# Small copies on VectorE in a two-layer hybrid attention block: products from PSUM, gathers on ScalarE

## The chip, the cores and the metric

One core of one Trainium2 chip runs the whole program. The metric is the time of one execution on the device in microseconds (us); the profile beside it comes from one further execution of the same program. Five engines work side by side, each through its own instructions in order: TensorE (PE, with PEld for its weight loads), VectorE (DVE), ScalarE (ACT), GpSimd (POOL) and SyncE (SP), which issues weight transfers.

## The reference

A block of two layers works on 272 tokens of width 1024, of which the first 16 ("meta" tokens) are prepended. Each layer has a mixer with three kinds of heads, and a feed-forward part:

```python
h = concatenate([meta, x])                      # 16 + 256 tokens, width 1024
for l in range(2):
    u = rmsnorm(h, norm_mix[l])
    qa, ka, va, qi, ki, wi, qb, kb, vb, qc, kc, vc, gc = split(u @ w_in[l])
    # a: 8 heads; an indexer (qi, ki, wi) picks the top 64 keys of each query; softmax; p @ va
    # b: 4 heads; two softmaxes of 32-wide halves, w = p0 - lam * p1; w @ vb; rmsnorm
    # c: 4 heads; rotary, then retention in chunks with decay; rmsnorm; times silu(gc)
    h = h + concatenate([a_out, b_out, c_out]) @ w_out[l]
    u = rmsnorm(h, norm_ff[l])
    h = h + square(relu(u @ w_ff1[l])) @ w_ff2[l]
return rmsnorm(h, final_norm)[:, 16:]
```

## The kernel before

The work is cut into units of one 1024x128 block of weights: per layer 31 units for w_in, 8 for w_out, 32 and 32 for the feed-forward part. One unit is one `slot`: 24 matmuls of 256 or 272 columns into one of four PSUM banks (`mm`). Each weight block comes by a transfer on SyncE's queue into `raw` (three buffers, five units ahead), is rounded by ScalarE into `hi` (L167, three units ahead), and the rest `raw - hi` goes into `lo` (L179, two units ahead), on VectorE or, for the units of `POOL_LO`, on GpSimd. The activations are split in the same way (`uh`, `ul`), so that each product is three matmuls (L186 to L188).

Everything else is set by hand into the gaps between the unit's matmuls. A slot has six places (evac, none, quarter, half, most, all); `PLACES` and `AFTER` give for each small function the slot and the place at which its instructions are put, as slot times six plus place. On each engine the instructions run in the order in which they are put.

Tokens lie along the columns; a tile of 128 partitions by 272 columns holds two heads of 64 (or four halves of 32). The first 16 columns belong to the meta tokens, and all heads' work on them is put together in block-diagonal form:

- `e_mul` (L464, L466) and `b_split` (L471) turn PSUM into `ka`, `qa`, `kb`, `qb` by the row factor `bcast[key]` (tile bc). In the first layer, `meta_softmax` has three steps: `one` copies the first 16 columns of each head into its block of `kmA` or `kmB` (L577, tiles cleared once on GpSimd at L352); `two` multiplies with the queries, adds the bias, and takes minimum, difference (L592) and exponential; `three` divides by the sum (L601).
- `e_v` makes `vt` from PSUM (L475) and copies the first 16 columns into the blocks of `vbdT` (L477, L478). `e_v2` transposes vt on TensorE (L487) and ScalarE empties the bank (L488).
- `e_rot` makes the rotated `kr` and `qr` (L500, L503 on VectorE, the sum at L504 on GpSimd), and `e_kbd` copies kr's first columns into the blocks of `kbdT` (L507, L508), which `c_meta` multiplies with qr (L760).
- `b_pair`, `b_norm`, `b_keys` and `b_keys2` run the b heads: softmax parts (VectorE L554, L555, ScalarE L557, L558), sums and their inverse (L706, L707), a scaling on GpSimd (tile bp, L709), the difference on VectorE (L714), then a copy of the map's columns for meta keys into `wm` (L720), and the transposes (L563) with ScalarE's copy of the bank (L564).
- `i_head`, `i_round` and `i_mask` (L538, L544, L546, L550) find the top 64 on VectorE. `a_bias` adds mask and bias on GpSimd (L617, L618), `a_pair` multiplies (L627), `a_norm` scales on ScalarE (L640), `a_keys` copies the meta columns into `pm` (L649) and transposes.
- `e_ki` makes `kf` (L429), a rounded copy `kh` of it by a cast (L430), and the rest (L433).

Of the kernel before, what the change touches and what calls it, by code (L numbers as in the profile page):

```python
# [8 lines left out]
F = mybir.dt.float32  # L9
R = mybir.dt.float32r  # L10
AF = mybir.ActivationFunctionType
OP = mybir.AluOpType
# [5 lines left out]
T = SEQ + NM  # L18
# [8 lines left out]
N_UNITS = N_IN + N_OUT + N_F1 + N_F2  # L27

C_ID, C_ONES, C_COS, C_SIN, C_NEG, C_DEC, C_DECM, C_EXP = 0, 128, 256, 528, 800, 1072, 2608, 2880
C_ALL = 2896  # L30
P_MIX, P_FF, P_DN, P_RN = 0, 16, 32, 34
P_ALL = 38

# [4 lines left out]
PLACES = {  # L38
    "i_head": (28, 28, 34, 39, 45, 44, 52, 45),
    "i_round": (55, 57, 62, 64, 74, 77, 86, 91),  # L40
    "i_mask": (101,),
    "b_pair": (70, 87),
    "b_norm": (78, 79, 92, 98),
    "b_keys": (80, 83, 93, 101),
    "b_keys2": (88, 90, 100, 109),
    "a_bias": (104, 104, 107, 113, 131, 132, 140, 145),
# [6 lines left out]
    "r_scale": (123, 179),  # L53
    "r_out": (130, 181),
    "rot_tables": (99,),
    "e_kbd": (146, 157),
    "c_pair": (158, 163),
    "c_meta": (162,),
    "a_meta": (169,),
    "e_wi2": (16,),  # L60
    "b_first": (91,),
    "b_soft": (76, 84, 86),
    "a_soft": (124, 130, 136),
    "a_pv": (175, 181, 187, 195),
    "factor": (11, 12, 17),
}

AFTER = {
# [29 lines left out]
def block_kernel(ctx: ExitStack, tc: tile.TileContext, W, hin, cst, onehot, rbe, par, fin, dlam, out):  # L98
    nc = tc.nc
    ctx.enter_context(tc.manual_schedule())  # L100
    V, S, G, PE = nc.vector, nc.scalar, nc.gpsimd, nc.tensor
# [5 lines left out]
    small = ctx.enter_context(tc.tile_pool(name="small", bufs=3))  # L107
# [113 lines left out]
    cs = const.tile([128, C_ALL], F, name="cs")  # L221
# [3 lines left out]
    z = const.tile([128, 128], F, name="z")  # L225
# [21 lines left out]
    dec = cs[:, C_DEC:C_DEC + 1536].rearrange("p (h c) -> p h c", h=4)  # L247
    decm = cs[:, C_DECM:C_DECM + T]
    nhalf = cs[:, C_EXP:C_EXP + 16]

    nb = const.tile([128, 12, T], F, name="nb")
    vbdT = const.tile([128, 8, 128], F, name="vbdT")
    kbdT = const.tile([128, 2, 32], F, name="kbdT")
    kmA = const.tile([128, 4, 32], F, name="kmA")
    kmB = const.tile([128, 2, 64], F, name="kmB")
    smT = const.tile([128, 2, T], F, name="smT")
# [37 lines left out]
    bcast = {}  # L294
# [53 lines left out]
    at(13, "all", late_constants)  # L348

    def clear():  # L350
        for z in (vbdT, kbdT, kmA, kmB, smT[64:128]):
            G.memset(z, 0.0)  # L352
        G.memset(ss, 1.0)

# [54 lines left out]
    def meta_cols(x):  # L409
        return x[:, 0:288].rearrange("p (t c) -> p t c", t=2)[:, :, 0:16]  # L410

    def mixer(l):
# [3 lines left out]
        first = l == 0  # L416
        st = {}
        key = ("bc", l)
        factor_to_rows(b, key, 0, False)

        def e_ki(ps):
            bc = bcast[key]
            f = ta("kf")
            k2 = ck([128, 2, T], R, "ki")
            kh, kl = k2[:, 0], k2[:, 1]
            V.tensor_tensor(f[64:128], ps[64:128, :T], bc[64:128], OP.mult)  # L429
            V.tensor_copy(kh[64:128], f[64:128])  # L430
            S.activation(kh[0:64], f[64:128], AF.Copy)
            for r in (slice(64, 128), slice(0, 64)):
                V.tensor_tensor(kl[r], f[64:128], kh[64:128].bitcast(F), OP.subtract)  # L433
            st["ki"] = kh, kl
# [23 lines left out]
        def e_mul(ps, name, m, n, n0, scale=None):  # L458
            bc = bcast[key]
            if name not in st:  # L460
                st[name] = ck([128, n, T], F, name)
            o = st[name][:, m, n0:]
            if scale is None:
                V.tensor_tensor(o, ps[:, n0:T], bc[:, n0:], OP.mult)  # L464
            else:
                V.scalar_tensor_tensor(o, ps[:, n0:T], scale, bc[:, n0:], OP.mult, OP.mult)  # L466

        def b_split(ps, name, m, n0, scale):
            if name not in st:
                st[name] = ck([128, 2, T], F, name)  # L470
            V.scalar_tensor_tensor(st[name][:, m, n0:], ps[:, n0:T], scale, bcast[key][:, n0:], OP.mult, OP.mult)  # L471

        def e_v(ps, name, c0, vs):
            vt = ta("vt")
            V.tensor_tensor(vt, ps[:, :T], bcast[key], OP.mult)  # L475
            c = 32 * (vs if vs < 4 else vs % 2)
            V.tensor_copy(vbdT[0:64, vs, c:c + 16], vt[0:64, 0:16])  # L477
            V.tensor_copy(vbdT[64:128, vs, c + 16:c + 32], vt[64:128, 0:16])  # L478
            st["vt", vs] = vt

        def e_v2(name, c0, vs):
# [14 lines left out]
        def e_rot(ps, name, m, n0):  # L496
# [5 lines left out]
                i, o = 32 * q, 32 * (q ^ 1)  # L502
                V.tensor_tensor(y[o:o + 32, n0:], ps[i:i + 32, n0:T], st["sinr"][i:i + 32, n0:], OP.mult)  # L503
            G.tensor_tensor(st[name][:, m, n0:], x[:, n0:], y[:, n0:], OP.add)  # L504

        def e_kbd(m):
            V.tensor_copy(kbdT[0:64, m, 0:16], st["kr"][0:64, m, 0:16])  # L507
            V.tensor_copy(kbdT[64:128, m, 16:32], st["kr"][64:128, m, 0:16])  # L508

        def e_gate(ps, m):  # L510
            if m == 0:
# [51 lines left out]
                PE.transpose(pt[:, a * 128:a * 128 + 128], p[:, c:c + 128], ident)  # L563
            S.activation(dst, pt[:, :384], AF.Copy)  # L564

        def meta_softmax(name, plan, q, k, km, bias):

            tiles = km.shape[1]
            per = 8 // tiles
            rows = 128 // per  # L570
            x = {}

            def one():
                for i in range(tiles):
                    for a in range(per):
                        r = slice(rows * a, rows * a + rows)
                        V.tensor_copy(km[r, i, 16 * a:16 * a + 16], st[k][r, i, 0:16])  # L577

            def two():
                ps = att()  # L580
                for i in range(tiles):
                    PE.matmul(ps[:16, i * per * 16:(i + 1) * per * 16], st[q][:, i, 0:16], km[:, i, :],
                              start=True, stop=True)
                t = ta("mt", (16, 8, 16))
                if bias.ndim == 4:
                    V.tensor_tensor(t.rearrange("p (h a) c -> p h a c", a=2),
                                    ps[:16, :128].rearrange("p (h a c) -> p h a c", a=2, c=16), bias, OP.add)
                else:
                    V.tensor_tensor(t, ps[:16, :128].rearrange("p (h c) -> p h c", c=16), bias, OP.add)
                mn = small.tile([16, 8], F, name="mmn", bufs=1)  # L590
                V.tensor_reduce(mn, t, AX.X, OP.min)
                V.tensor_tensor(t, t, mn[:, :, None].to_broadcast([16, 8, 16]), OP.subtract)  # L592
                S.activation(t, t, AF.Exp, scale=-1.0)
                x["t"] = t

            def three():
                t = x["t"]
                sm = small.tile([16, 8], F, name="msm", bufs=1)
                V.tensor_reduce(sm, t, AX.X, OP.add)
                V.reciprocal(sm, sm)  # L600
                V.tensor_tensor(t, t, sm[:, :, None].to_broadcast([16, 8, 16]), OP.mult)  # L601
                st[name] = t

            for p, f in zip(PLACES[plan], (one, two, three)):
                place(b, p, f)

        def meta_v(name, vs, n):
# [34 lines left out]
        def a_keys(hd):  # L642
            if hd == 0:
                st["pm"] = wk([128, 2, 8, 16], "pm")
                st["pT"] = []
            if hd % 2 == 0:
                st["pT"].append(ck([128, 2, 384], F, "pT"))
            t = st.pop(("a", hd))
            V.tensor_copy(st["pm"][:, :, hd, :], meta_cols(t))  # L649
            to_keys(t, st["pT"][hd // 2][:, hd % 2, :])  # L650

        def a_meta():
# [58 lines left out]
        def b_keys(hd):  # L711
            (w, p1), sm, e = st.pop(("b", hd))
            for t, sl in enumerate((T0, T1)):
                V.scalar_tensor_tensor(w[:, sl], e[:, sl], sm[:, t:t + 1], p1[:, sl], OP.mult, OP.subtract)  # L714
            if hd == 0:
                st["wm"] = wk([128, 2, 4, 16], "wm")
                st["wT"] = []
            if hd % 2 == 0:
                st["wT"].append(ck([128, 2, 384], F, "wT"))
            V.tensor_copy(st["wm"][:, :, hd, :], meta_cols(w))  # L720
            st["w", hd] = w

        def b_keys2(hd):
# [121 lines left out]
        units += [("gc", m) for m in range(2)] + [("va", m) for m in range(4)]  # L845
        full = ("ki", "vb", "kb", "ka", "vc", "kr", "va")

        for f in (e_wi2, i_mask, b_meta, rot_tables, c_meta, a_meta):
            place(b, PLACES[f.__name__][0], f)
        for f in (i_head, i_round, b_pair, b_norm, b_keys, b_keys2, a_bias, a_pair, a_norm, a_keys,  # L850
                  r_pv, r_norm, r_scale, r_out, e_kbd, c_pair):
            for a, p in enumerate(PLACES[f.__name__]):
                place(b, p, f, a)
        if first:
            meta_softmax("bmeta", "b_soft", "qb", "kb", kmB,
                         nb[0:16, 8:12, None, 144:160].to_broadcast([16, 4, 2, 16]))
            place(b, PLACES["b_first"][0], b_first)
            meta_softmax("ameta", "a_soft", "qa", "ka", kmA, nb[0:16, 0:8, 144:160])

        def after(i, f, *a):  # L860
            place(i, AFTER[f.__name__], f, *a)
# [1 line left out]
        for u, (kind, *m) in enumerate(units):  # L863
            m = m[0] if m else 0
            i = b + u
# [253 lines left out]
def _constants(np):  # L1119
# [12 lines left out]
    for hd in range(4):  # L1132
# [2 lines left out]
        c[:, C_DEC + 384 * hd:C_DEC + 384 * hd + 256] = g(q0 - p)  # L1135
        c[:, C_DEC + 384 * hd + 256:C_DEC + 384 * hd + 384] = g(q1 - p)
        c[16 * hd:16 * hd + 16, C_DECM:C_DECM + T] = g(q - np.arange(16)[:, None])
    c[:, C_EXP:] = -0.5
    dist = 271 - np.arange(400)
    n = np.maximum(dist, 0)  # L1140
    nf = np.maximum(n, 1).astype(np.float32)
# [69 lines left out]
```

## Time and profile before

| | |
|---|---|
| median of 3 runs | 741.5 us (740.35 to 743.11) |
| the profiled execution's own time | 742.43 us |
| span of its instructions | 740.6 us |
| mean granted clock of TensorE | 0.981 |
| busy: PE, PEld | 710.3 us (96%), 666.3 us (90%) |
| busy: DVE, ACT, POOL | 495.2 us (67%), 374.5 us (51%), 163.8 us (22%) |
| transfers | 115.53 MB, mean 156 GB/s |

Busy times are from one profiled execution. Matmuls are pipelined, so that a busy PE is not PE at its peak. The granted clock is the share of TensorE's 2.4 GHz that the chip allowed in a stretch. A bracket behind an instruction says how long its engine stood idle before it and which instruction ended that; "L" is the line of the kernel. Times in a row are its start and its duration, counted from the start of the span.

### The profile page before, as it was taken

What the parts mean: (1) busy time and instruction counts of PE and PEld (TensorE: products, weight loads), DVE (VectorE), ACT (ScalarE), POOL (GpSimd) and SP (SyncE); (2) the same over time, 40 slices, a digit from 0 to 9 for tenths busy, and PEclk for the clock granted to TensorE, in tenths of its full rate; (3) what the DMA queues carried; (4) which work ended last, traced back from release to release, by engine and by line L of the source; (5) the groups of instructions that cost most, each with busy time, mean ns of one, the idle gap of its engine ahead of it and who ended that gap; (6) DMA issues with size and microseconds to landing.
All of it is one profiled execution on the core that took longest, in us unless ns stands there. A gap on an engine that the chain in (4) does not pass through costs nothing.

```text
span 740.6 us, 13376 instructions
## 1 busy us (share of the span) xinstructions
PE 710.3 (96%) x5248; PEld 666.3 (90%) x5248; DVE 495.2 (67%) x970; ACT 374.5 (51%) x695; POOL 163.8 (22%) x139
## 2 busy tenths in 40 slices
PE   8998899899999999999999998989999999999996
PEld 7987788789999999999999987978899998998995
DVE  6679869865877666464646897697486555555554
ACT  6425555435556555343435556553376445545543
POOL 3537544213200000000004758340140000000000
PEclk9999999899999999999999999998999999999998
DMA  7586323224545555646453533332356555555551
GB/s 233 140 223 219 97 105 108 77 76 141 191 155 195 171 171 172 190 156 195 156 187 114 176 121 117 108 107 86 114 170 221 178 186 196 188 177 206 186 171 57
DMA packets 34403, 115.53 MB, mean 156 GB/s; under 512 B 3971, under 2 KB 6308, under 8 KB 34340
## 3 DMA queue, kind: packets, MB, share of 16 engines
q1 hardware_dynamic: 31824, 111.00, 45.2%
q10 hardware_dynamic: 2516, 3.68, 2.4%
q8 instruction: 41, 0.67, 0.4%
q14 instruction: 22, 0.18, 0.1%
HBM read 113.00 MB, written 1.66 MB: 155 GB/s over the span
## 4 chain that ended last, share of the span: by engine, by line
PE 75%; DVE 15%; issue 3%; POOL 3%; DMA 3%; ACT 1%; SPq 0%; POOLq 0%; ACTq 0%; DVEq 0%
PE mm L186 19%; PE mm L188 19%; PE mm L187 18%; PE att L977 11%; DMA raw<-w 2%; DVE lo L179 2%; DVE acc L546 1%; DVE ry L503 1%; DVE m L544 1%; DVE wm L720 1%; POOL lo L179 1%; PE att L780 1%; DMA h<-hin 1%; DVE bp L555 1%; DVE kmB L577 1%
## 5 line engine op out<-in xcount | busy, mean ns | idle before, releaser
L167 ACT ACTIVATE hi<-raw 128x1024 fp32r<-128x1024 f32 x204 | 214.7, 1056 | 186.9 <-PE mm L187 133.0
L186 PE MATMUL mm<-uh,hi 128*128 128x272 f32 (+1 forms) x1008 | 298.6, 296 | 2.5 <-DVE ka L464 2.0
L188 PE MATMUL mm<-uh,lo 128*128 128x272 f32 (+1 forms) x1008 | 292.2, 290 | 3.5 <-POOL lo L179 2.7
L187 PE MATMUL mm<-ul,hi 128*128 128x272 f32 (+1 forms) x1008 | 291.1, 289 | 0.4
L179 DVE TENSOR_TENSOR lo<-raw,hi 128x1024 fp32r<-128x1024 f32 (+1 forms) x172 | 210.9, 1245 | 22.4 <-ACT hi L167 21.6
L186 PEld LDWEIGHTS mm<-uh,hi 128*128 128x128 f32 x1008 | 193.4, 192 | 10.1 <-issue 5.4
L188 PEld LDWEIGHTS mm<-uh,lo 128*128 128x128 f32 x1008 | 193.0, 191 | 5.0 <-POOL lo L179 3.6
L187 PEld LDWEIGHTS mm<-ul,hi 128*128 128x128 f32 x1008 | 193.6, 192 | 2.8 <-DVE ul L268 1.4
L179 POOL TENSOR_TENSOR lo<-raw,hi 128x1024 fp32r<-128x1024 f32 x36 | 87.8, 2447 | 75.7 <-ACT hi L167 63.3
L186 PE MATMUL mm<-sh,hi 128*128 128x272 f32 x256 | 74.2, 290 | 0.0
L188 PE MATMUL mm<-sh,lo 128*128 128x272 f32 x256 | 74.1, 289 | 0.0
L187 PE MATMUL mm<-sl,hi 128*128 128x272 f32 x256 | 73.7, 288 | 0.0
L276 POOL TENSOR_TENSOR sacc<-sacc,sq 128x272 f32<-128x272 f32 (+1 forms) x24 | 23.0, 957 | 206.4 <-ACT sq L274 206.1
L960 DVE TENSOR_TENSOR fr<-fr 128x256 f32<-128x256 f32 x32 | 13.6, 425 | 58.2 <-ACT fr L959 58.2
L187 PEld LDWEIGHTS mm<-sl,hi 128*128 128x128 f32 x256 | 48.3, 188 | 0.0
L186 PEld LDWEIGHTS mm<-sh,hi 128*128 128x128 f32 x256 | 48.2, 188 | 0.0
L188 PEld LDWEIGHTS mm<-sh,lo 128*128 128x128 f32 x256 | 48.2, 188 | 0.0
L1016 POOL TENSOR_TENSOR nr<-nv,cs 128x1 f32<-128x1 f32 x2 | 1.1, 561 | 178.9 <-DVE nv L1014 178.9
L977 PE MATMUL att<-hi,sh 128*128 128x512 f32 x128 | 40.2, 394 | 0.0
L977 PE MATMUL att<-hi,sl 128*128 128x512 f32 x128 | 40.2, 394 | 0.0
L186 PE MATMUL mm<-oh,hi 128*128 128x272 f32 (+1 forms) x128 | 36.9, 289 | 0.0
L187 PE MATMUL mm<-ol,hi 128*128 128x272 f32 (+1 forms) x128 | 36.6, 286 | 0.0
(237 smaller groups left out, 963.1 us busy)
## 6 DMA issues: line engine op xcount, KB each, us to landing
raw<-w SPq DMA_DIRECT2D x204, 512.0 KB, 3.6
nb<-scr ACTq DMA_DIRECT2D x4, 408.0 KB, 6.6
h<-hin SPq DMA_DIRECT2D x4, 272.0 KB, 4.7
raw<-w SPq DMA_DIRECT2D x4, 256.0 KB, 4.3
out_dram<-fo SPq DMA_DIRECT2D x4, 256.0 KB, 2.2
cs<-cst ACTq DMA_DIRECT2D x1, 904.0 KB, 5.6
scr<-row ACTq DMA_DIRECT2D x1, 600.0 KB
fg<-fin SPq DMA_DIRECT2D x1, 512.0 KB, 5.1
```

The lines of the kernel that those rows point to most:

```text
L167: S.activation(hi[:, p], raw[:, p], AF.Copy)
L179: eng.tensor_tensor(lo[:, p], raw[:, p], hi[:, p].bitcast(F), OP.subtract)
L186: PE.matmul(ps, hi[:, k, :], xh, start=first and j == 0, stop=False)
L187: PE.matmul(ps, hi[:, k, :], xl, start=False, stop=False)
L188: PE.matmul(ps, lo[:, k, :], xh, start=False, stop=last and j == len(ks) - 1)
L276: eng.tensor_tensor(sacc[part][:, q0:], sacc[part][:, q0:], sq[:, q0:], OP.add)
L503: V.tensor_tensor(y[o:o + 32, n0:], ps[i:i + 32, n0:T], st["sinr"][i:i + 32, n0:], OP.mult)
L544: V.max(m, acc[:, sl])
L546: V.match_replace(acc[:, sl], m, acc[:, sl], MARK)
L555: V.tensor_tensor_reduce(t[:, T1], ps[:, T1], bias1, 1.0, 3.0e38, OP.add, OP.min, mn[:, 1:2])
L960: V.tensor_tensor(r[:, q0:], r[:, q0:], r[:, q0:], OP.mult)
L977: PE.matmul(acc[t, a], x, w[part][:, 512 * a:512 * a + 512], start=k == 0 and x is xh and part == 0, stop=k == 31 and part == 1)
```

## The change

The block-diagonal tiles are no longer filled by copies. `block_factors` makes two tiles per layer, the row factor of the first 16 tokens times a block mask of zeros and ones, and `blocks_of` multiplies PSUM with one of them; the tile is written whole, so that kmA, kmB and kbdT need no clearing. kbdT is made on GpSimd from kr and the mask. The columns for `wm` and `pm` are gathered by ScalarE. Of meta_softmax step `one` is gone, `two` and `three` stand at earlier places (b: 74 and 84 in place of 84 and 86; a: 124 and 136 in place of 130 and 136), and the difference and the last product run on GpSimd. kh is made from PSUM by a product.

```diff
-    "e_kbd": (146, 157),
-    "b_soft": (76, 84, 86),
-    "a_soft": (124, 130, 136),
+    "b_soft": (74, 84),
+    "a_soft": (124, 136),
+    "block_factors": (24,),
...
+    mask2 = cs[:, C_M2:C_M4].rearrange("p (a c) -> p a c", a=2)
+    mask4 = cs[:, C_M4:].rearrange("p (a c) -> p a c", a=4)
...
-        for z in (vbdT, kbdT, kmA, kmB, smT[64:128]):
+        for z in (vbdT, smT[64:128]):
...
+        def block_factors():
+            for n, mask in ((2, mask2), (4, mask4)):
+                f = small.tile([128, n, 16], F, name="bf%d" % n, bufs=1)
+                V.tensor_tensor(f, mask, bcast[key][:, None, 0:16].to_broadcast([128, n, 16]), OP.mult)
+                st["bf", n] = f
+
+        def blocks_of(dst, ps, n):
+            V.tensor_tensor(dst.rearrange("p (a c) -> p a c", a=n), ps[:, None, 0:16].to_broadcast([128, n, 16]),
+                            st["bf", n], OP.mult)
...
-            V.tensor_copy(kh[64:128], f[64:128])
+            V.tensor_tensor(kh[64:128], ps[64:128, :T], bc[64:128], OP.mult)
...
                 V.tensor_tensor(o, ps[:, n0:T], bc[:, n0:], OP.mult)
+                if first:
+                    blocks_of(kmA[:, m], ps, 2)
...
+            if first and name == "kb":
+                blocks_of(kmB[:, m], ps, 4)
...
-            V.tensor_copy(vbdT[0:64, vs, c:c + 16], vt[0:64, 0:16])
-            V.tensor_copy(vbdT[64:128, vs, c + 16:c + 32], vt[64:128, 0:16])
+            blocks_of(vbdT[:, vs, c:c + 32], ps, 2)
...
-        def e_kbd(m):
-            V.tensor_copy(kbdT[0:64, m, 0:16], st["kr"][0:64, m, 0:16])
-            V.tensor_copy(kbdT[64:128, m, 16:32], st["kr"][64:128, m, 0:16])
+            if name == "kr":
+                G.tensor_tensor(kbdT[:, m].rearrange("p (a c) -> p a c", a=2),
+                                st[name][:, m, None, 0:16].to_broadcast([128, 2, 16]), mask2, OP.mult)
...
-            def one():
-                for i in range(tiles):
-                    for a in range(per):
-                        r = slice(rows * a, rows * a + rows)
-                        V.tensor_copy(km[r, i, 16 * a:16 * a + 16], st[k][r, i, 0:16])
...
-                V.tensor_tensor(t, t, mn[:, :, None].to_broadcast([16, 8, 16]), OP.subtract)
+                G.tensor_tensor(t, t, mn[:, :, None].to_broadcast([16, 8, 16]), OP.subtract)
...
-                V.tensor_tensor(t, t, sm[:, :, None].to_broadcast([16, 8, 16]), OP.mult)
+                G.tensor_tensor(t, t, sm[:, :, None].to_broadcast([16, 8, 16]), OP.mult)
...
-            V.tensor_copy(st["pm"][:, :, hd, :], meta_cols(t))
+            S.activation(st["pm"][:, :, hd, :], meta_cols(t), AF.Copy)
...
-            V.tensor_copy(st["wm"][:, :, hd, :], meta_cols(w))
+            S.activation(st["wm"][:, :, hd, :], meta_cols(w), AF.Copy)
...
-    c[:, C_EXP:] = -0.5
+    c[:, C_EXP:C_M2] = -0.5
+    c[:, C_M2:C_M4] = p // 64 == np.arange(32)[None, :] // 16
+    c[:, C_M4:] = p // 32 == np.arange(64)[None, :] // 16
```

## Rows read from the trace of the kernel before

**Rows 1.** Busy us (instructions) by engine, granted clock, DMA share, GB/s, both mixers.

```profile
40.00:182.00 142.00, 129.09 (x953) 115.32 (x953) 109.34 (x307) 69.55 (x165) 57.53 (x45) 0.95 0.40 128
404.00:532.00 128.00, 120.10 (x942) 111.17 (x940) 100.03 (x272) 68.71 (x160) 60.57 (x46) 0.96 0.35 116
```

**Rows 2.** The same view (PE, PEld, DVE, ACT, POOL), two stretches inside the mixers.

```profile
60.00:80.00 20.00, 17.97 (x136) 16.69 (x134) 19.46 (x61) 11.09 (x35) 10.65 (x8) 0.91 0.56 193
480.00:500.00 20.00, 17.00 (x139) 15.49 (x137) 19.54 (x47) 11.63 (x31) 8.62 (x9) 1.00 0.31 106
```

**Rows 3.** PE's timeline: start, us, instruction, idle before and its releaser.

```profile
74.31 0.36 PE L186 MATMUL mm<-uh,hi 128*128 128x272 f32 x1 [1.99 <-DVE ka L464]
...
81.95 0.30 PE L563 MATMUL att<-cs,bp 128*128 128x128 f32 x1 [1.99 <-DVE bp L714]
...
93.97 0.85 PE L563 MATMUL att<-cs,ap 128*128 128x128 f32 x3 [0.86 <-ACT ap L640]
...
114.66 1.38 PE L627 MATMUL att<-ka,qa 64*128 64x144 f32 x8 [1.12 <-DVE ol L831]
...
137.54 0.62 PE L760 MATMUL att<-qr,kbdT 128*32 128x272 f32 x2 [2.34 <-DVE kbdT L508]
...
430.02 0.41 PE L487 MATMUL att<-cs,vt 128*128 128x128 f32 x2 [1.00 <-DVE vt L475]
...
459.18 0.90 PE L563 MATMUL att<-cs,ap 128*128 128x128 f32 x3 [2.10 <-ACT ap L640]
...
500.23 0.59 PE L760 MATMUL att<-qr,kbdT 128*32 128x256 f32 x2 [2.99 <-DVE kbdT L508]
```

**Rows 4.** Busy us by engine and granted clock (third number from the end), four stretches.

```profile
84.00:88.00 4.00, 3.73 (x18) 3.21 (x18) 3.81 (x10) 0.29 (x1) 3.07 (x4) 0.57 0.41 133
138.00:146.00 8.00, 7.68 (x33) 6.75 (x33) 6.23 (x12) 3.02 (x6) 0.00 (x0) 0.57 0.19 66
459.00:464.00 5.00, 4.73 (x24) 3.94 (x25) 1.71 (x2) 3.11 (x8) 3.01 (x3) 0.66 0.36 116
500.00:508.00 8.00, 7.45 (x32) 6.41 (x33) 6.14 (x13) 2.48 (x6) 0.05 (x1) 0.57 0.20 66
```

**Rows 5.** Chain that ended last, 56 to 75 us: start, us, what.

```profile
62.00 2.33 DVE kmB L577
...
69.77 1.63 DVE wm L720
...
71.93 1.88 DVE mt L592
```

**Rows 6.** POOL's timeline, four places of both mixers.

```profile
59.59 4.72 POOL L179 TENSOR_TENSOR lo<-raw,hi 128x1024 fp32r<-128x1024 f32 x2 [0.22 <-ACT hi L167]
...
92.07 0.50 POOL L617 TENSOR_TENSOR ap<-mask,nb 128x144 f32<-128x144 f32 x1
...
135.01 2.35 POOL L179 TENSOR_TENSOR lo<-raw,hi 128x1024 fp32r<-128x1024 f32 x1
...
497.03 0.72 POOL L504 TENSOR_TENSOR qr<-ra,ry 128x256 f32<-128x256 f32 x1 [3.86 <-DVE ry L503]
```

**Rows 7.** DVE's timeline, three copies.

```profile
135.09 2.29 DVE L508 COPY kbdT<-kr 64x16 f32<-64x16 f32 x1
...
424.59 2.35 DVE L478 COPY vbdT<-vt 64x16 f32<-64x16 f32 x1
...
447.66 1.82 DVE L720 COPY wm<-bp 128x32 f32<-128x32 f32 x1
```

**Rows 8.** DVE's groups by line and shape: count, busy us, mean ns, idle before.

```profile
L720 DVE COPY wm<-bp 128x32 f32<-128x32 f32 x8 | 11.2, 1394 | 0.3
...
L446 DVE COPY wi<-att 128x16 f32<-128x16 f32 x2 | 0.3, 174 | 0.1
```

**Rows 9.** ACT's groups by line and shape.

```profile
L640 ACT ACTIVATE ap<-ap,sm 128x272 f32<-128x272 f32 x16 | 8.1, 507 | 0.0
...
L640 ACT ACTIVATE ap<-ap,sm 128x144 f32<-128x144 f32 x16 | 6.5, 408 | 13.0 <-DVE sm L638 12.9
```

More of the change, by code (lines that the diff above doesn't have):

```diff
@@ L29 @@
 C_ID, C_ONES, C_COS, C_SIN, C_NEG, C_DEC, C_DECM, C_EXP = 0, 128, 256, 528, 800, 1072, 2608, 2880
-C_ALL = 2896
+C_M2, C_M4, C_ALL = 2896, 2928, 2992
 P_MIX, P_FF, P_DN, P_RN = 0, 16, 32, 34
@@ L564, in to_keys, with meta_softmax @@
             S.activation(dst, pt[:, :384], AF.Copy)
-        def meta_softmax(name, plan, q, k, km, bias):
+        def meta_softmax(name, plan, q, km, bias):
             tiles = km.shape[1]
             per = 8 // tiles
-            rows = 128 // per
             x = {}
-            def one():
-                for i in range(tiles):
-                    for a in range(per):
-                        r = slice(rows * a, rows * a + rows)
-                        V.tensor_copy(km[r, i, 16 * a:16 * a + 16], st[k][r, i, 0:16])
             def two():
@@ L600, in three @@
                 V.reciprocal(sm, sm)
-                V.tensor_tensor(t, t, sm[:, :, None].to_broadcast([16, 8, 16]), OP.mult)
+                G.tensor_tensor(t, t, sm[:, :, None].to_broadcast([16, 8, 16]), OP.mult)
                 st[name] = t
-            for p, f in zip(PLACES[plan], (one, two, three)):
+            for p, f in zip(PLACES[plan], (two, three)):
                 place(b, p, f)
@@ L846, in mixer @@
         full = ("ki", "vb", "kb", "ka", "vc", "kr", "va")
-        for f in (e_wi2, i_mask, b_meta, rot_tables, c_meta, a_meta):
+        for f in (block_factors, e_wi2, i_mask, b_meta, rot_tables, c_meta, a_meta):
             place(b, PLACES[f.__name__][0], f)
         for f in (i_head, i_round, b_pair, b_norm, b_keys, b_keys2, a_bias, a_pair, a_norm, a_keys,
-                  r_pv, r_norm, r_scale, r_out, e_kbd, c_pair):
+                  r_pv, r_norm, r_scale, r_out, c_pair):
             for a, p in enumerate(PLACES[f.__name__]):
@@ L854, in mixer @@
         if first:
-            meta_softmax("bmeta", "b_soft", "qb", "kb", kmB,
+            meta_softmax("bmeta", "b_soft", "qb", kmB,
                          nb[0:16, 8:12, None, 144:160].to_broadcast([16, 4, 2, 16]))
             place(b, PLACES["b_first"][0], b_first)
-            meta_softmax("ameta", "a_soft", "qa", "ka", kmA, nb[0:16, 0:8, 144:160])
+            meta_softmax("ameta", "a_soft", "qa", kmA, nb[0:16, 0:8, 144:160])
         def after(i, f, *a):
```

## The prediction

> **What bounds the kernel now.** I read the busy shares by stage first, then TensorE's own timeline for its idle time, then the granted clock around it, and last the chain of waits with the timelines of VectorE and GpSimd, to see who was late. Three of the five stages (start, feed-forward of the first layer, last feed-forward) run with TensorE filled; only the two mixers, 40 to 182 us and 404 to 532 us, hold TensorE idle: 129.09 of 142 us and 120.10 of 128 us busy, at granted clocks of 0.95 and 0.96 [rows 1]. Inside them VectorE is close to full, 19.46 and 19.54 of 20 us in the worst stretches, while ScalarE has 8 to 9 us of each 20 free and GpSimd more still [rows 2]. So a mixer's limit is partly TensorE's work and partly VectorE being late.
>
> TensorE's long waits in the mixers that I think this change can touch are eight [rows 3]: 1.99 at 74.31, 1.99 at 81.95, 0.86 at 93.97, 1.12 at 114.66, 2.34 at 137.54, 1.00 at 430.02, 2.10 at 459.18, 2.99 at 500.23, in sum 14.39 us. I leave out those under half a microsecond, and one near 58 us behind a lo on GpSimd, to which no copy leads.
>
> Four of these waits are followed by a stretch at the lower clock level, 1.2 GHz in place of 2.4. The mean granted clock was 0.57 in 84 to 88, 0.57 in 138 to 146, 0.66 in 459 to 464, 0.57 in 500 to 508 us [rows 4]. The clock time missing is 0.43x4 + 0.43x8 + 0.34x5 + 0.43x8 = 10.3 us. Before each, TensorE had stood idle for 1.99 to 2.99 us; the other four waits, one of 1.99 us among them, are followed by none, so a wait makes such a stretch likely, not certain.
>
> Who was late: the chain of waits goes through the copies themselves. One of the eight kmB copies takes 2.33 us, a wm copy 1.63, the subtraction on mt 1.88 [rows 5], for 16 to 128 columns. The timelines show why. GpSimd's weight subtractions (tile lo) start at 59.59 and run back to back for 4.72 us, and the kmB copy that starts at 62.00 ends at 64.33, with the second of them. The lo that starts at 135.01 and takes 2.35 ends at 137.36 [rows 6]; the kbdT copy issued at 135.09 takes 2.29 and ends at 137.38 [rows 7], and the first wait of [rows 3] that names kbdT ends there. The vbdT copy of 2.35 us at 424.59 and the wm copy of 1.82 at 447.66 [rows 7] are of the same kind. An SBUF copy on VectorE is held until GpSimd's running instruction ends.
>
> **The change part by part.** (a) kmA, kmB and vbdT: 16 small copies in the first mixer and 16 per layer go. In their place stands one product per unit (4, 2 and 8 of them) that reads PSUM and a small factor of 32 or 64 columns. No row has just this; a 16-column read from PSUM took 174 ns [rows 8], and I take 0.2 us each, so 22 x 0.2 = 4.4 us over both layers. Only one operand lies in SBUF, as with the PSUM products around them, and I count on no hold. It lengthens the use of the PSUM bank by the same 0.2 us, hidden behind the four banks in rotation.
>
> (b) The factors themselves: two products of SBUF operands per layer, early in unit 4. That stretch has no listed wait, and 0.4 us there I cost at nothing; had GpSimd a lo running, each could be held by one lo, 2.4 us, and the first i_head sums behind them would be late.
>
> (c) wm and pm move to ScalarE: eight wm copies at a mean of 1394 ns [rows 8] and sixteen pm copies leave VectorE, and 24 copies of 32 columns join ScalarE. There 144 columns took 408 ns and 272 took 507 [rows 9], so by the slope 32 take about 0.32 us, 7.7 us in all, and between nothing and 0.41 each is the bound. Most falls in ScalarE's free time [rows 2]. But a_keys puts its gather before the copy that empties the transposes' bank, so up to 16 x 0.32 = 5.1 us could reach TensorE; with ScalarE a little over half busy I take a quarter, 1.2 us of loss.
>
> (d) kbdT moves to GpSimd, behind the rotary addition in e_rot, and mt's subtraction and product move too: four and four instructions. GpSimd's 144-column product took 0.50 us [rows 6], so at most 4 us, on an engine with room. kbdT is then there long before c_meta asks for it. The next late thing at c_meta is qr: in the second layer it is finished at 497.03 + 0.72 = 497.75, half a microsecond after TensorE's earlier end at 500.23 - 2.99 = 497.24, so that of 2.99 about 2.4 are won; in the first layer the same addition was done before the wait began.
>
> (e) e_ki's cast becomes a second product from PSUM. It stands near no listed wait: nothing. The masks make an early constant transfer longer by 48 KB: nothing either, and a few tenths lost at worst if the first weights come later. The memsets that go stand near no listed wait.
>
> (f) meta_softmax is moved earlier. The subtraction queues on GpSimd between two lo's and ScalarE's exp waits for it. Behind that exp stands a hi conversion that TensorE wants about three units later, so I cost it at nothing.
>
> Now the waits, in the order of [rows 3]. At 74.31 TensorE wants a bank that VectorE frees late, behind kmB, wm and mt: all of it, 2.0. At 81.95 the bp chain, by then 2.33 + 1.63 + 1.88 = 5.8 us late from the three instructions of [rows 5] alone: 1.7. At 93.97 the a_bias chain, which begins with the mask after a wm copy: 0.5. At 114.66 behind kmA: 0.8. At 137.54 kbdT: 2.2. At 430.02 vt behind the held vbdT copy: 0.9. At 459.18 the a_bias chain behind the wm copy at 447.66: 1.5, since a lo on GpSimd also stands in it. At 500.23: 2.4. Sum 12.0 of 14.39; the lower bound is the four that a held copy makes directly (74.31, 137.54, 430.02, 500.23), 7.5.
>
> The clock: between nothing and 10.3 us. After the two kbdT waits I take three quarters of 6.88, 5.2, for the wait goes almost whole; after the other two 0.6 of 3.42, 2.0. Sum 7.2.
>
> Together 12.0 + 7.2 - 1.2 = 18.0 us. The profiled execution took 742.4 us, so 724.4; the median of the runs is 0.9 us under it, and I forecast **723.5 us**.
>
> One rule goes beyond the copies. The Trainium skill (SBUF — State Buffer, section "Who interferes with whom") says that VectorE and GpSimd share one pair of SBUF ports, exclusively and for a whole instruction, and that a VectorE instruction with two SBUF inputs contends for it too when GpSimd reads SBUF. The 1.88 us of mt's subtraction, which has two SBUF inputs, agrees with that. By it the gain would shrink by what the new GpSimd work holds, to 727.5 us in place of 723.5; the second rival works that out from rows.
>
> **The rivals.** First, the next wait takes over: the a_bias and bp chains still hold GpSimd's lo's and ScalarE's exponentials, so only the direct 7.5 us go and the clock falls as before: 742.4 - 7.5 - 0.9 = 734 us. For it speaks that a lo of 2.35 us stands in the chain before 459.18; against it that VectorE is by then 2.35 + 1.82 = 4.2 us ahead from the two copies of [rows 7] alone.
>
> Second, the hold moves: the eight new GpSimd instructions read two SBUF tiles, and VectorE's remaining subtractions of two SBUF inputs are held by them as mt was. At 0.50 us each that is 4.0 us, 727.5. Against it: they are short and rarely meet one.
>
> Third, slower: ScalarE's wm gather in b_keys waits in order for VectorE's bp, with exponentials and the hi conversions behind it. Before, ScalarE had no instruction at that place. If each of the eight is held by a lo and a bp pair, 2.35 + 0.85 = 3.2 us, and all of it reaches TensorE, that is 25.6 us: 723.5 + 25.6 = 749. It decides from 2.7 us per gather on. Against it: hi is made about three units ahead of its use.
>
> Fourth, nothing to measure: TensorE's work is the pace, and its waits come back elsewhere within 3.7 us (0.5%, about what can be told from no change): 740.
>
> **Chances.** The forecast's case 0.62 (716 to 729), next wait 0.19 (730 to 737), moved hold 0.07, nothing 0.06, slower 0.06. Faster is the first three, 0.88. The lowest time is all of 14.39 + 10.3 = 24.7 us won, 742.4 - 24.7 - 0.9 = 716.8, and 2.8 us allowed for the shorter waits that I left out: 714. The range goes from there to 735, inside the next-wait case.
>
> **What would show it.** Right: no wait on kbdT at c_meta in either layer and a granted clock near 1 behind it; no PE wait on ka near 74; VectorE's busy time lower by clearly more than the 8 x 1.394 = 11.2 us of the wm copies alone, all of it in the mixers; ScalarE's higher by 7 to 8; the feed-forward stages as long as before. Wrong: a PE wait on ScalarE's hi or pT, ScalarE waiting for VectorE's bp at the gathers, lo subtractions on VectorE well over their usual time, or low clock behind waits of another make.

## The result, and the profile after

The changed kernel took **718.08 us** (median of 4 runs, 717.73 to 718.95) against 741.4 us before (4 runs, 740.35 to 743.11). The ratio is 0.9685, 95% interval 0.9665 to 0.9705: 23.3 us faster, by the ratio 21.9 to 24.8 us. The forecast was 723.5 us, range 714 to 735. The profiled execution has a span of 716.3 us against 740.6 before.

The two mixers at the times of [rows 1], the two stretches round c_meta, then the stretches of the mixers whose clock is still low (PE, PEld, DVE, ACT, POOL; the granted clock is the third number from the end):

```profile
40.00:182.00 142.00, 137.02 (x1074) 125.31 (x1073) 104.86 (x284) 79.98 (x191) 66.56 (x57) 0.99 0.45 146
404.00:532.00 128.00, 125.33 (x1018) 116.71 (x1016) 92.75 (x250) 74.64 (x181) 58.96 (x52) 0.99 0.39 132
...
120.00:136.00 16.00, 15.76 (x121) 13.48 (x119) 13.72 (x29) 8.29 (x22) 3.10 (x2) 1.00 0.32 100
470.00:490.00 20.00, 19.24 (x154) 17.52 (x153) 17.07 (x38) 10.71 (x28) 4.87 (x5) 1.00 0.33 107
...
56.00:66.00 10.00, 8.08 (x52) 7.43 (x51) 8.72 (x35) 8.39 (x24) 9.42 (x9) 0.83 0.48 166
436.00:450.00 14.00, 12.24 (x89) 11.18 (x89) 5.01 (x22) 9.50 (x29) 6.92 (x9) 0.88 0.42 146
```

TensorE's idle time in the first pair fell from 12.91 + 7.90 = 20.81 us to 4.98 + 2.67 = 7.65, so 13.2 us less, and the clock rose from 0.95 and 0.96 to 0.99. (The work slides forward: the stretches hold somewhat more of the next stage than before, but that stage has next to no idle time.) The stretch 56 to 66 is not new; the kernel before has the same there, behind a wait of 1.92 us at 59.42 on the same lo:

```profile
56.00:66.00 10.00, 8.08 (x50) 7.67 (x50) 9.86 (x33) 8.41 (x23) 7.08 (x3) 0.83 0.51 179
```

Ahead of the mixers, the profile after also has a granted clock of 0.79 over 5 to 13 us, behind a wait of 1.43 us at 6.24 for the first hi; before it is 1.00, with 0.23 us waited. That leaves no loss: the third unit begins at 17.0 us in both.

The time is won in the mixers: the 77 units from the first layer's w_out on take 237.1 us before (167.8 to 404.9) and 237.2 after (152.3 to 389.5).

TensorE's timeline in the mixers, with its waits of over half a microsecond:

```profile
50.13 0.44 PE L503 MATMUL att<-cs,vt 128*128 128x128 f32 x2 [0.87 <-DVE vt L492]
...
58.12 0.39 PE L188 MATMUL mm<-uh,lo 128*128 128x272 f32 x1 [1.92 <-POOL lo L179]
...
85.94 0.85 PE L578 MATMUL att<-cs,ap 128*128 128x128 f32 x3 [1.33 <-ACT ap L648]
...
440.10 0.93 PE L578 MATMUL att<-cs,ap 128*128 128x128 f32 x3 [1.67 <-ACT ap L648]
...
479.82 0.92 PE L757 MATMUL att<-qr,kr 64*128 64x256 f32 x6 [0.76 <-ACT vm L620]
```

Six of the eight waits are gone (ka, bp, ol, vt and both kbdT). The two before the probabilities' transposes (ap) are not: 0.86 became 1.33 and 2.10 became 1.67. Of 14.39 us, 14.39 - 1.33 - 1.67 = 11.4 are won. The waits on vm, 0.76 us (in the first mixer 0.24), and on vt at 50.13, 0.87 us, are new; that of 0.85 us on acc at 43.88, which [rows 3] do not list, is gone.

Who now takes what (VectorE, ScalarE, GpSimd by line and shape: count, busy us, mean ns, idle before):

```profile
L431 DVE TENSOR_TENSOR vbdT<-mm,bf 128x32 f32<-128x32 f32 x16 | 2.9, 182 | 0.0
...
L427 DVE TENSOR_TENSOR bf<-cs,bc 128x64 f32<-128x64 f32 x2 | 2.6, 1319 | 0.0
...
L446 DVE TENSOR_TENSOR ki<-kf,ki 64x272 fp32r<-64x272 f32 x4 | 3.8, 956 | 0.1
...
L715 DVE TENSOR_SCALAR bsm<-bsm,lam 128x2 f32<-128x2 f32 x8 | 5.9, 738 | 0.3
...
L657 ACT ACTIVATE pm<-ap 128x32 f32<-128x32 f32 x16 | 3.5, 216 | 0.0
...
L728 ACT ACTIVATE wm<-bp 128x32 f32<-128x32 f32 x8 | 1.8, 226 | 5.2 <-DVE bp L722 5.2
...
L522 POOL TENSOR_TENSOR kbdT<-kr,cs 128x32 f32<-128x32 f32 x4 | 4.5, 1115 | 0.3
...
L600 POOL TENSOR_TENSOR mt<-mt,mmn 16x128 f32<-16x128 f32 x2 | 0.8, 392 | 1.6 <-DVE mmn L599 1.6
```

The products from PSUM are short and none is held. Some VectorE instructions from SBUF are held now that were not: two of the four rests of ki (0.96 us in the mean; 0.44 before), the product of bsm with lam, two columns, in four of its eight places (0.74 us in the mean and 0.23 before), and the wider factor bf in the first layer. Its mean of 1.32 us is one value of 2.42 and one of 0.22; the pair of factors took

```profile
27.94 2.53 DVE L427 TENSOR_TENSOR bf<-cs,bc 128x32 f32<-128x32 f32 x2
...
387.99 0.33 DVE L427 TENSOR_TENSOR bf<-cs,bc 128x32 f32<-128x32 f32 x2
```

with a lo on GpSimd from 28.01 to 30.40 beside the first pair and none beside the second. VectorE's busy time over the execution fell from 495.2 to 463.0 us: by 18.3 and 16.3 us in the two mixers, while the start rose by 1.7.

### The profile page after: what moved, and what is told of

It reads as the page before. It is cut to its first block, busy times and chain, and to the rows that moved or that the text cites. A ratio compares the mean times of both kernels' runs of the same rounds, so it can differ in the third digit from the quotient of the medians.

```text
span 716.3 us, 13333 instructions
## 1 busy us (share of the span) xinstructions
PE 698.8 (98%) x5248; PEld 659.1 (92%) x5248; DVE 463.0 (65%) x912; ACT 377.5 (53%) x719; POOL 167.1 (23%) x144
## 4 chain that ended last, share of the span: by engine, by line
PE 77%; DVE 10%; POOL 4%; DMA 3%; issue 2%; ACT 2%; SPq 0%; ACTq 0%; POOLq 0%; DVEq 0%
PE mm L186 19%; PE mm L188 19%; PE mm L187 19%; PE att L985 12%; DMA raw<-w 2%; DVE lo L179 2%; POOL lo L179 2%; DVE ry L519 2%; DVE ul L270 1%; PE att L788 1%; ACT hi L167 1%; DMA h<-hin 1%; PE att L782 1%; DVE acc L561 1%; ACT ap L648 1%
## 5 line engine op out<-in xcount | busy, mean ns | idle before, releaser
L179 DVE TENSOR_TENSOR lo<-raw,hi 128x1024 fp32r<-128x1024 f32 (+1 forms) x172 | 214.8, 1267 | 22.4 <-ACT hi L167 21.4
```

What stands on the lines that cost most here:

```text
L179: eng.tensor_tensor(lo[:, p], raw[:, p], hi[:, p].bitcast(F), OP.subtract)
```

## The experiments

The theory: VectorE's SBUF copies cost what they do because they are held while GpSimd runs a lo or another of its instructions, and the held ones make TensorE wait; the low clock is what follows such a wait. The rivals: VectorE simply had too many instructions; the low clock comes from the light matmuls at c_meta, not from the wait; and the last two waits come from another instruction that is now held (bsm), or from GpSimd's own lo. In experiments that edit the kernel before or after, line numbers move by a few; the tiles' names tell what is what.

**e1: kernel before, kbdT alone on GpSimd.**

```
-        def e_kbd(m):
-            V.tensor_copy(kbdT[0:64, m, 0:16], st["kr"][0:64, m, 0:16])
-            V.tensor_copy(kbdT[64:128, m, 16:32], st["kr"][64:128, m, 0:16])
+            if name == "kr":
+                G.tensor_tensor(kbdT[:, m].rearrange("p (a c) -> p a c", a=2),
+                                st[name][:, m, None, 0:16].to_broadcast([128, 2, 16]), mask2, OP.mult)
...
```

> The kernel before, with kbdT alone made on GpSimd from kr and a mask. Theory (held copies make the waits, and the waits bring the low clock): the waits of 2.34 us at 137.5 and 2.99 us at 500.2 go but for some 0.5, 4.8 us, and with them the low clock behind them, 5 to 6.9 us: 730 to 732 us. Rival (the clock is low there for the light attention matmuls, not for the wait): only 4 to 5 us, 736 to 738, with the clock of 138 to 146 still near 0.57.

Measured: 732.77 us, just above the theory's range and well under the rival's; ratio 0.9873 [0.9834, 0.9911], 9.4 us of 741.4. Both kbdT waits are gone, and the stretches round c_meta in either layer show:

```profile
130.00:146.00 16.00, 15.91 (x122) 13.69 (x121) 14.23 (x31) 7.96 (x20) 3.11 (x2) 1.00 0.31 100
480.00:510.00 30.00, 29.23 (x234) 26.14 (x233) 26.98 (x59) 14.70 (x34) 9.97 (x11) 1.00 0.31 106
```

The granted clock is 1.00 where [rows 4] have 0.57 in the second half of each. The matmuls there are those of before; only the idle time ahead of them went. So the low clock came with the wait and not from light work. The mean granted clock of its four executions is 0.992 to 0.994, that of the seven of the kernel before beside them 0.976 to 0.989. The waits on the other tiles stay about as they were (2.11 us at 75.03 for ka, 1.98 at 82.68 for bp, 2.08 at 454.55 for ap): each is its own loss. New is one of 2.29 us at 47.71 on a lo of VectorE, which takes back a part of the gain.

**e2: kernel before, every small copy left on VectorE but written as a sum over an axis of length one.**

```
+    def move(dst, src):
+        if len(src.shape) == 2:
+            V.tensor_reduce(dst, src[:, :, None], AX.X, OP.add)
+        else:
+            V.tensor_reduce(dst, src[:, :, :, None], AX.X, OP.add)
...
-            V.tensor_copy(st["wm"][:, :, hd, :], meta_cols(w))
+            move(st["wm"][:, :, hd, :], meta_cols(w))
```

(and so for vbdT, kbdT, kmA, kmB and pm)

> The kernel before, with each of the small VectorE copies (kmA, kmB, vbdT, kbdT, wm, pm) written as a VectorE sum over an axis of length one: same instructions in number, place, engine and bytes, but no longer an SBUF copy. Theory (a copy is held by GpSimd's instruction, another form of one SBUF input is not): each takes 0.2 to 0.25 us wherever it stands, and most of the gain comes, 719 to 726 us; mt's subtraction and the cast stay as they were. Rival (it is the number and place of small VectorE instructions that makes it late): 738 us or more.

Measured: 721.12 us, ratio 0.9711 [0.9677, 0.9745]. VectorE's groups:

```profile
L411 DVE TENSOR_REDUCE vbdT<-vt 64x16 f32<-64x16 f32 x32 | 5.2, 164 | 0.8
...
L413 DVE TENSOR_REDUCE wm<-bp 128x32 f32<-128x32 f32 x8 | 1.5, 186 | 0.3
...
L411 DVE TENSOR_REDUCE kmB<-kb 32x16 f32<-32x16 f32 x8 | 1.3, 159 | 0.1
L411 DVE TENSOR_REDUCE kbdT<-kr 64x16 f32<-64x16 f32 x8 | 1.2, 154 | 0.1
```

The same moves, in the same places on the same engine, with the same count: wm takes 186 ns in place of the 1394 of [rows 8], and the longest of the others are gone with it. By the ratios that is 0.0289 of 0.0315, 92% of what the whole change brings. The count of VectorE's instructions is not the cause; what the copies are held by is. In the trace before, 27 of the 80 copies take 0.27 to 2.35 us, and each of them ends within 0.05 us behind the end of a GpSimd instruction (14 of a lo, 7 of an a_bias addition, 4 of a rotary addition, 2 of a bp scaling); the other 53 take 0.16 to 0.18 us. The Trainium skill (SBUF — State Buffer, section "Who interferes with whom") says that a copy can take the port pair shared with GpSimd and that a reduction never does on this chip: the trace agrees, with means of 154 to 186 ns for the sums. In one thing the hold is narrower than the prediction has it: eight vbdT copies of the kernel before start while GpSimd computes the power hv (8 or 12 columns, 1.65 to 2.29 us, as at 104.92) and take 0.17 us all the same. Why hv holds none was not tried.

**e3 to e6: the changed kernel with one part undone.** e3 puts the wm gather back on VectorE, e4 the pm gather, e5 the vbdT copies, e6 the kmA and kmB copies at the head of meta_softmax.

```
# e3
-            S.activation(st["wm"][:, :, hd, :], meta_cols(w), AF.Copy)
+            V.tensor_copy(st["wm"][:, :, hd, :], meta_cols(w))
# e4
-            S.activation(st["pm"][:, :, hd, :], meta_cols(t), AF.Copy)
+            V.tensor_copy(st["pm"][:, :, hd, :], meta_cols(t))
# e5
-            blocks_of(vbdT[:, vs, c:c + 32], ps, 2)
+            V.tensor_copy(vbdT[0:64, vs, c:c + 16], vt[0:64, 0:16])
+            V.tensor_copy(vbdT[64:128, vs, c + 16:c + 32], vt[64:128, 0:16])
# e6 (and kmA, kmB cleared at the start)
...
-                    blocks_of(kmA[:, m], ps, 2)
...
-                blocks_of(kmB[:, m], ps, 4)
...
             def two():
+                rows = 128 // per
+                for i in range(tiles):
+                    for a in range(per):
+                        r = slice(rows * a, rows * a + rows)
+                        V.tensor_copy(km[r, i, 16 * a:16 * a + 16], st["k" + q[1]][r, i, 0:16])
```

> The changed kernel with the eight wm copies put back on VectorE. Theory: they are held again, 1.4 us each and 11 us in all, in the stretch where VectorE is fullest, and some of the waits at bp and in the a_bias chain come back: 721 to 726 us. Rival (instruction count): eight instructions of 0.2 us, 718 to 719.

> The changed kernel with the sixteen pm copies put back on VectorE. Theory: before, their mean was 346 ns, most of them not held, so little is lost, 718 to 720 us. Rival (instruction count, or ScalarE better placed): twice as many instructions as wm, so a greater loss than with wm.

> The changed kernel with vbdT filled again by two VectorE copies from vt per unit. Theory: most of these copies meet no GpSimd instruction (before, 32 of them took 8.5 us), so only the one or two that do are held; the wait at vt in the second mixer comes back in part, 718 to 720 us. Rival (number of instructions): 16 more of them than the products, like e4.

> The changed kernel with kmA and kmB filled again by copies, at the head of step two, in the first mixer only. Theory: the eight kmB copies are held by the lo's of GpSimd as before, some 4 to 5 us, and VectorE falls behind where the first mixer is fullest: 720 to 724 us, all of it in the first mixer. Rival (VectorE now has slack enough to hide them): 718.

| kernel | us | ratio to before, interval | lost against the change (0.9685) |
|---|---|---|---|
| e3, wm on VectorE | 724.93 | 0.9758 [0.9724, 0.9792] | 0.0073 = 5.4 us |
| e4, pm on VectorE | 719.42 | 0.9682 [0.9645, 0.9719] | none |
| e5, vbdT copies | 720.08 | 0.9707 [0.9680, 0.9734] | 0.0022 = 1.6 us |
| e6, kmA, kmB copies | 723.28 | 0.9746 [0.9713, 0.9779] | 0.0061 = 4.5 us |

In e3, the gather's group on VectorE, and TensorE's wait in the second mixer:

```profile
L728 DVE COPY wm<-bp 128x32 f32<-128x32 f32 x8 | 11.2, 1406 | 0.3
```

```profile
447.06 1.10 PE L578 MATMUL att<-cs,ap 128*128 128x128 f32 x3 [2.11 <-ACT ap L648]
```

The changed kernel has 1.67 there, so this wait is only a part of the loss. In the first mixer the wait on ap is 1.98 us at 89.15 in place of 1.33, and now a low clock follows it (0.57 over 89 to 93).

In e4 some pm copies are held as well, and TensorE's waits on ap stay at 1.32 and 1.70 us:

```profile
L657 DVE COPY pm<-ap 128x32 f32<-128x32 f32 x16 | 8.4, 528 | 1.9 <-ACT ap L648 1.9
```

In e5, TensorE's timeline has a wait on vt like that at 430.02 in [rows 3]; in e6, one at kmB (and one of 1.52 us at 104.40 at kmA):

```profile
417.39 0.41 PE L504 MATMUL att<-cs,vt 128*128 128x128 f32 x2 [1.59 <-DVE vt L492]
```

```profile
61.17 0.37 PE L591 MATMUL att<-kmB,qb 128*16 128x64 f32 x2 [2.53 <-DVE kmB L588]
```

With e1 the parts sum to 9.4 + 5.4 + 4.5 + 1.6 + 0 = 20.9 of 23.3 us; as e1 starts from the kernel before and the others from the changed one, that they should add up is not shown. Each ratio is known to 0.003 or 0.004 (2 to 3 us), so e5's 1.6 alone is no loss that could be told from none: its wait is in the trace, its price is not settled. For pm, 8.4 us of copies cost nothing that can be told from none, and no wait of TensorE grew by more than 0.03 us.

**e7 and e8: the two waits that are left.** The chain of waits of the changed kernel, ahead of the second one (start, us, what):

```profile
429.66 1.42 DVE bsm L715
431.08 0.34 DVE cosr L509
431.42 0.35 DVE sinr L510
431.78 0.40 DVE mask L565
...
432.50 2.08 POOL lo L179
...
434.83 1.48 POOL ap L625
```

Two suspects stand in it: the held product of two columns (bsm), and unit 18's lo, which sits on GpSimd between the mask and the a_bias additions. e7 takes the first away; e8 does so and moves that lo to VectorE.

```
# e7 and e8
-            V.tensor_scalar(sm[:, 2:4], sm[:, 2:4], lam[:, l:l + 1], None, OP.mult)
...
-                G.tensor_scalar(p[1][:, sl], p[1][:, sl], sm[:, 2 + t:3 + t], 0.0, OP.mult, OP.add)
+                G.tensor_scalar(p[1][:, sl], p[1][:, sl], sm[:, 2 + t:3 + t], lam[:, l:l + 1], OP.mult, OP.mult)
# e8 only
-POOL_LO = (5, 6, 7, 8, 10, 11, 12, 13, 14, 15, 16, 17, 18, 20, 24, 28, 34, 36)
+POOL_LO = (5, 6, 7, 8, 10, 11, 12, 13, 14, 15, 16, 17, 20, 24, 28, 34, 36)
```

> The changed kernel, and lam is no longer multiplied into the sums on VectorE (a product of two columns by a scalar, SBUF to SBUF, 1.38 and 1.42 us on the chains before the two longest waits left) but is the second scalar of the scaling on GpSimd that follows. Theory (such a product is held like a copy): the a_bias chains shorten by 1.2 us each, the waits of 1.33 and 1.67 us shrink to under 0.5, and with the second its low clock goes: 714 to 716 us. Rival (the lo on GpSimd between mask and a_bias sets those waits): 717 to 719.

> As e7, and the weight rest lo of unit 18, which stands on GpSimd between the mask and a_bias, is made on VectorE (1.25 us there, 2.4 on GpSimd). Theory and rival of e7 agree here: both waits at the first a_keys go, 712 to 715 us; above 717 if VectorE, given 1.25 us more per layer at its fullest, falls behind again.

e7 took 718.48 us, ratio 0.9684 [0.9658, 0.9711]: nothing won, as the rival had it. Its waits on ap are 1.89 and 1.71 us. Its chain, in the first mixer:

```profile
75.25 0.09 DVE bsm L714
75.34 1.70 DVE cosr L509
77.04 0.35 DVE sinr L510
77.39 0.30 DVE mask L565
...
78.40 1.80 POOL lo L179
...
80.70 1.48 POOL ap L625
```

The hold did not go, it passed to the next VectorE instruction with two SBUF inputs (cosr, 1.70 us where it had taken 0.34), and the mask ended where it had. e8 took 713.98 us, ratio 0.9627 [0.9601, 0.9654].

**e9 and e10: the lo's alone.** e9 is the changed kernel with the second edit of e8 alone. e10 is e8 with unit 12's lo on VectorE too, aimed at the 1.92 us at 58.12.

> The changed kernel with one edit: the fp32r rest of unit 18's weights is subtracted on VectorE instead of GpSimd, where it stands between the a_bias mask on VectorE and the a_bias additions on GpSimd (78.36, 2.03 us and 432.50, 2.08 us). Theory (this rest alone sets the last two waits, of 1.33 and 1.67 us): the waits go, and with them some 1.5 us of missing clock at 436 to 450: 718.1 - 3.0 - 1.5 = 713.6 us, the same as with both edits. Rival (the held product with lam and the rest set them together, one after the other): without the lam edit 0.7 to 1.3 us stay at each place, 715.5 to 717 us.

> The best kernel so far (lam on GpSimd, unit 18's rest on VectorE) with unit 12's rest on VectorE too. It aims at the wait of 1.92 us at 58.73, for a rest of unit 12 that ends on GpSimd at 58.68, and at the low clock behind it (0.83 over 56 to 66, 1.7 us). Theory: the rest on VectorE ends about 1.2 us after its start and the wait falls to 0.5 us or less; with a part of the clock, 714.0 - 1.5 - 0.5 to 1.7 = 711 to 712 us. Rival: VectorE, which at that place is in the b_pair row minima until 57.5, starts the rest as late, and everything behind it on VectorE moves 1.2 us; the wait stays above 1 us or turns up at the next product: 713.5 to 715 us.

e9 took 714.49 us (713.75 to 715.39, 5 runs), ratio 0.9621 [0.9592, 0.9649], as fast as e8. Its timeline of TensorE at the two places, and the stretch whose clock had been 0.88:

```profile
85.01 0.85 PE L578 MATMUL att<-cs,ap 128*128 128x128 f32 x3 [0.26 <-ACT ap L648]
...
437.94 0.85 PE L578 MATMUL att<-cs,ap 128*128 128x128 f32 x3 [0.41 <-ACT ap L648]
```

```profile
436.00:450.00 14.00, 13.51 (x111) 12.55 (x110) 6.54 (x22) 10.86 (x32) 6.67 (x8) 1.00 0.32 113
```

So the lo alone set these waits, and the product with lam, though still held (0.72 us in the mean), cost nothing. e9 differs from the changed kernel by one entry of a list and is 3.6 us faster by the medians, 4.7 by the ratios, whose intervals do not meet.

e10 took 716.66 us, ratio 0.9642 [0.9614, 0.9671], above what theory and rival gave; its median is 2.7 us above e8's and 2.2 above e9's, but the intervals overlap, so it is shown to win nothing and not shown to lose. TensorE's and VectorE's timelines and the stretch's row, from the slowest of its five executions, say why nothing is won:

```profile
59.71 0.66 PE L503 MATMUL att<-cs,vt 128*128 128x128 f32 x2 [4.37 <-DVE vbdT L431]
```

```profile
56.74 1.23 DVE L179 TENSOR_TENSOR lo<-raw,hi 128x1024 fp32r<-128x1024 f32 x1 [4.50 <-ACT hi L167]
```

```profile
56.00:66.00 10.00, 6.29 (x30) 5.88 (x31) 8.80 (x42) 8.33 (x23) 4.05 (x3) 0.66 0.43 160
```

The lo is made in 1.23 us, but VectorE takes its work in order and stood 4.50 us for ScalarE's hi, with vt and vbdT behind it. TensorE's wait grew from 1.92 to 4.37 us. What is late there is hi, and an engine that waits for it should be one with nothing urgent behind.

## Why the prediction was right, point by point

The mechanism was as forecast: held copies, waits behind them, low clock behind the waits. The sizes differ in both directions.

- **The waits: 12.0 us forecast, 11.4 measured.** That the sum is close is luck: two errors offset each other. The waits behind ka, bp, ol, vt and the two kbdT, put at 10.0 us together, went whole: 11.43. The two of the a_bias chain, put at 0.5 and 1.5, gave -0.47 and 0.43. There the first rival was right: the next in the chain, a lo on GpSimd, took over, as e9 shows. The argument against it, that VectorE is 4.2 us ahead, missed that GpSimd takes that lo before the additions, so that the additions wait for its end and not for the mask alone. At the second kbdT I named qr as late next, at half a microsecond; what came was vm, 0.76 us a step later, so 2.99 - 0.76 = 2.2 us are won there, near the 2.4 put down, for another reason.
- **The clock: 7.2 us forecast of 10.3; 8.6 measured in its four stretches.** Three of the four stretches of [rows 4] are whole again; the fourth, behind the a_bias wait, has its twin at 436 to 450: 0.12 x 14 = 1.7 us. That is 8.6 us. e1 shows that it goes with the wait. The shares of three quarters and 0.6 were too careful where a wait went whole, and too high where it stayed. A fifth low stretch of the kernel before, 56 to 66, was left out with its wait, rightly: it is there after as well. The low clock is partly luck of the execution: in e4 and e5 the a_bias waits in the second mixer, 1.70 and 1.86 us, were followed by a clock of 1.00, where the changed kernel's profile lost 1.7 us behind 1.67.
- **ScalarE's gathers: 1.2 us of loss forecast, none seen.** They take 216 and 226 ns, not 320, 5.3 us in all and not 7.7. ScalarE waits for bp 5.2 us in sum at the wm gathers, which is the third rival's place, but no wait of TensorE over half a microsecond can be laid to it: the one on vm, which ScalarE makes, is 0.77 us in e1 too, where no gather is on ScalarE, and e4, without the pm gathers, is no faster.
- **The sum.** With the sizes found it is 11.4 + 8.6 = 20.0 us against 18.0 forecast, where the span fell by 24.3. Of the rest, 13.2 - 11.4 = 1.8 us are shorter idle times in the mixers, which I had left out, less the new waits on vm and vt. Some 2.5 us lie in no idle time and no low clock of these stretches, so TensorE counts as busy in both kernels there; they stay unassigned.
- **The products (0.2 us)** were right: 182 ns for vbdT. That an operand in PSUM keeps them clear of the hold was right too: none of the 22 took over 0.22 us, several of them beside a lo.
- **The factors at nothing** were right in the price: the wider one was held as feared by one lo, 2.42 us, in the first layer alone, and no wait of TensorE over half a microsecond follows.
- **GpSimd's eight new instructions at 0.50 us at most** failed for kbdT: 1.12 us for 32 columns, more than twice the bound, which came from an addition of plain columns. Both kbdT waits went all the same.
- **The moved hold**, second rival: it did move, to bsm, ki and bf, by more than the 4.0 us put there: 8 x (0.738 - 0.229) + 4 x (0.956 - 0.439) + (2.42 - 0.2) = 8.4 us of VectorE, and its own lo's took 3.9 us more in sum (1267 ns in the mean in place of 1245). But the holders are GpSimd's lo's, scalings and additions that were there before, not the eight new instructions, as far as the timelines show. Two of VectorE's lo's took 2.61 and 2.64 us, at 79.16 and 433.31, beside the lo that e9 moves: one of the signs set for being wrong did show. The rival's price was wrong in the other direction: none of it was seen to reach TensorE, and for bsm e7 shows that taking it away changes nothing.
- **The rule read from the rows**, that an SBUF copy is held until GpSimd's running instruction ends, holds for 27 copies and fails for the eight beside hv (e2).
- **The signs:** VectorE's busy time fell by 32.2 us, over the 11.2 set, and the fall lies in the mixers; no wait on kbdT or ka is left, and the stages between the mixers take as long as before. ScalarE's busy time rose by 3.0 us, under the 7 to 8.

## What to carry to other kernels

When a small instruction's mean is many times what its columns need, look at what the neighbour engine was doing at its start and end; the gain is in the hold and in the wait behind it, not in the instruction count. Writing such a copy in a form that isn't held (a product from PSUM, a sum over an axis of length one) recovers it without moving work to another engine. And price a removed wait by asking what else stands in its chain: a hold can pass to the next instruction from SBUF, and a long subtraction queued between two links of the chain sets the time however early the first link ends.

## What the runs showed of the hardware that was not expected

- A sum over an axis of length one moves 16 to 32 columns in 154 to 186 ns beside a busy GpSimd (e2), where the copies took up to 2.35 us [rows 7].
- A product of two columns took 1.42 us in the chain above, and 1.38 in the first mixer; with that one gone (e7), a product of 272 columns took 1.70 there. Each ends just behind the lo beside it, bsm by 0.03 us and the other by 0.3.
- GpSimd took 1.12 us for kbdT's 128 x 32 with the first operand repeated over a middle axis, against 0.39 us for 16 x 128 (mt). Whether the repeat or the short rows of 16 cost it was not tried.
- A TensorE wait of 1.92 us at 58.12 was followed by a clock of 0.83 over 56 to 66, one of 1.33 us at 85.94 by 1.00 over 86 to 90, and one of 1.67 us at 440.10 by 0.88 over 436 to 450. In e7 the first of them, again 1.92 us, at 58.88, was followed by 1.00 over 56 to 66. The length of a wait alone does not say which, and the same wait need not have the same price twice.
